# Longer expected waits around the decay products of the gated delta rule

## The chip, the core and the metric

The kernel runs on one core of one Trainium2 chip. TensorE multiplies matrices into PSUM; VectorE (DVE), ScalarE (ACT) and GpSimd (POOL) do the elementwise work; SyncE (SP) issues the loads. The engines run side by side and wait for one another on semaphores, and each takes its own instructions in the order in which the program lists them. The metric is the device time of one execution in microseconds (us), lower is better.

## The reference, cut to what matters

Two transformer blocks run on 512 tokens of width 1024 in float32. The first block mixes tokens with four groups of heads (softmax attention with a forget gate, gated delta rule, and two gated linear attentions), then a gated feed-forward; the second holds a short convolution, latent attention and two more feed-forwards. The change touches the gated delta rule:

```
G = jnp.cumsum(g.reshape(b, h, n, c), axis=-1)
decay = jnp.exp(jnp.where(causal, G[..., :, None] - G[..., None, :], -jnp.inf))
m = jnp.where(strict, jnp.einsum('bhnrd,bhnsd->bhnrs', kb, k) * decay, 0.0)
t_mat = m + jnp.eye(c, dtype=m.dtype)
w = lax.linalg.triangular_solve(t_mat, kb * jnp.exp(G)[..., None], ...)
u = lax.linalg.triangular_solve(t_mat, v * beta[..., None], ...)
a_qk = jnp.where(causal, jnp.einsum('bhnrd,bhnsd->bhnrs', q, k) * decay, 0.0)
```

After that a state of 64x64 per head goes from chunk to chunk. There are four heads, worked in two pairs.

## The kernel before, in words

All weights are float32 and are split into a high and a low part, so that a product is three matmuls per slice of 128 inputs (high by high, high by low, low by high). Such a triple is called a dense step here; a dense product of 128 output columns is eight of them. The token mixing stage takes the first 409 us and has 37 dense products: 29 that make the inputs of the heads (one of 29 named jobs each) and 8 of the output projection. It holds 296 dense steps, and between them stand the small matmuls of the heads.

TensorE's order in this stage is written by a planner in the kernel, `conduct` (L761). It runs once, when the program is built. Three lanes hold the heads' work as generators: lane G (the delta rule's pairs, here gdn0 and gdn1; PSUM tiles `gps`), lane L (hg0, gla, hg1: the gated linear attentions; `lps`) and lane F (fox0, fox1: softmax attention; `fps`). A generator issues some work and yields the time, by the planner's own clock, after which its next piece is expected to be ready. `conduct` adds the cost of every matmul that it writes to its clock. When a generator is due, its next piece is written; until then dense steps are. So a larger yield means that more dense steps stand between two pieces. The constants are LA = 0.68 and LV = 1.0 for one operation of ScalarE or VectorE. At run time the order is fixed, and a piece that is not ready holds up everything behind it on TensorE.

The order of VectorE, ScalarE and GpSimd is made by a scheduler from the same program, so it moves with TensorE's.

`gdn(p)` is the generator of one pair. It transposes k and q (L1059), then for each head j of the pair it writes the decay product (a masking matmul with `identb`, and four of `g` against a triangle, into one `gps` tile; the line of all `mm` calls is L708), ScalarE's exponential (tile `gmt`, L1091), the product of k and q and its weighting by VectorE (tile `gat`, L1034), the product of k and k and its weighting (`gmt`, L1034), and the start of the inverse (`u` L1113, `gxt` L1114). `gps` has two buffers. After both heads come six levels of block inversion (tiles `gy`, `gx`, `gxt`) and the chunk states (`gst`). `la` (L1325) is the generator body of lane L: seven levels, each with two copies per head into `lat` (L1371), products into `lbd` (L1320) and matmuls `lps<-lbd,lw`.

Three more rules matter. A job can be held until another piece is over: gv1, gk1 wait for gdn0's first half, gq1 for all of gdn0. Where a held job is not free, the next free one of the list is taken. And sigmoid-weighted inputs and gates (`silus`, L912) are collected, and a table load with a batch of activations follows only at jobs marked with a star in the list of jobs; gv1 has no star.

Of the kernel before, what the change touches and what calls it, by code (L numbers as in the profile page):

```python
# [648 lines left out]
LA, LV, LP = 0.68, 1.0, 1.5  # L649
# [17 lines left out]
class Mix(Mla):  # L667
# [371 lines left out]
    def gdn(self, p):  # L1039
# [34 lines left out]
        nc.vector.tensor_tensor(out=kof, in0=kof, in1=ik, op=ALU.mult)  # L1074
        nk = self.s1(8, "gnk", 2)
        nc.vector.tensor_tensor(out=nk, in0=ss[:, 8:16], in1=rr[:, 8:16], op=ALU.mult)
        yield 0.0
        MT, MR, AT, X, XT = [], [], [], [], []
        for j in range(2):
            rows = slice(64 * j, 64 * j + 64)  # L1080
            gp = self.pst()
            self.mm(c4(gp), self.identb, bc(self.negt), stop=False)
            for c in range(4):
                col = 4 * c + 2 * p + j
                self.mm(
                    gp[:, c * 128 : c * 128 + 128], self.g[:, col : col + 1].to_broadcast([128, 128]), self.triu,
                    start=False, stop=(c == 3),
                )
            e = self.b("gmt", bufs=2)
            for c in range(4):  # L1090
                nc.scalar.activation(  # L1091
                    out=e[:, c * 128 : c * 128 + 128], in_=gp[:, c * 128 : c * 128 + 128], func=ACTF.Exp,
                    bias=bias[:, 2 * c + j : 2 * c + j + 1],
                )
            yield Y_GDN / (1 + j)
            kp = self.pst()
            for c in range(4):
                cs = slice(c * 128, c * 128 + 128)
                self.mm(kp[:, cs], k[rows, cs], q[rows, cs])
            at = self.b("gat", bufs=2)  # L1100
            self.weighted(at, kp, ik, j, e)
            yield LV
            kp = self.pst()
            for c in range(4):
                cs = slice(c * 128, c * 128 + 128)
                self.mm(kp[:, cs], k[rows, cs], k[rows, cs])
            mt = e
            self.weighted(mt, kp, ik, j, e)
            mr = self.b("gmr", F32R, bufs=2)
            nc.scalar.activation(out=mr, in_=mt, func=ACTF.Copy)  # L1110
            xt = self.b("gxt", F32R, bufs=2)
            t1 = self.t(tag="s")
            nc.vector.tensor_tensor(out=c4(t1), in0=c4(mt), in1=bc(self.nm1), op=ALU.mult)  # L1113
            nc.vector.tensor_tensor(out=c4(xt), in0=c4(t1), in1=bc(self.ident), op=ALU.add)  # L1114
            MT.append(mt), MR.append(mr), AT.append(at), XT.append(xt)
            yield LV
        nc.gpsimd.tensor_tensor(out=d4(ke), in0=d4(ko), in1=b64(eG), op=ALU.mult)
        nc.gpsimd.tensor_tensor(out=d4(ko), in0=d4(ko), in1=b64(h2(kof)), op=ALU.mult)
        tp = self.to_tokens(v)
# [578 lines left out]
```

## Time and profile before

| what | value |
|---|---|
| median of three runs | 1855.37 us (1853.81 to 1861.0) |
| the profiled execution | 1864.82 us, span 1863.0 us |
| TensorE busy | 1825.5 us, 98% of the span |
| VectorE, ScalarE, GpSimd busy | 1051.9, 736.6, 190.3 us |
| mean granted TensorE clock | 0.989 |

The profile is one execution. A time in it is counted from the start of the span; "idle before" is the time that an engine stood still ahead of an instruction, with the instruction that released it; the granted clock is a share of TensorE's full speed of 2.4 GHz, so 0.50 is 1.2 GHz. Busy time of TensorE includes the modelled end of a matmul, which overlaps the next one, so the cost of a matmul in a stream is read from one start to the next.

### The profile page before, as it was taken

The page shows a single profiled execution, that of the slowest core. Times are in us where ns is not written, and L with a number is a line of the kernel's source. Part 1 is how long each engine was busy: PE and PEld are TensorE (multiplying, and loading weights), DVE is VectorE, ACT ScalarE, POOL GpSimd, SP SyncE. Part 2 cuts the span into 40 slices and gives each one's busy share as a digit, 9 for nine tenths or more (in the row PEclk, how much of TensorE's full clock was granted, in tenths as well). Part 3 has the DMA queues.
Part 4 walks back from the last instruction along what each step waited for, and adds up shares of the span by engine and source line. Part 5 has one row for each costly group of instructions (what it writes and reads, how often), then busy time and mean ns, then how long its engine had stood idle before and what let it go on. Part 6 is the DMA issues. An engine that isn't in the chain of part 4 may idle for free.

```text
span 1863.0 us, 22029 instructions
## 1 busy us (share of the span) xinstructions
PE 1825.5 (98%) x8609; PEld 1509.5 (81%) x8609; DVE 1051.9 (56%) x1620; ACT 736.6 (40%) x1138; POOL 190.3 (10%) x221
## 2 busy tenths in 40 slices
PE   8999999999999999999999999999999999999997
PEld 6787788878888888888888888888787888888886
DVE  7885966767777733455464444333876454444323
ACT  6544525554444422322342332222667433232322
POOL 1511402210000001011200000011011200000000
PEclk9999979999999999999999999999999999999999
DMA  4111101232222333222322222333222222222332
GB/s 167 57 46 35 57 23 35 97 99 102 91 102 92 96 94 95 99 102 91 102 96 102 91 101 92 93 101 98 70 61 74 79 91 102 95 98 92 100 94 76
DMA packets 53175, 162.61 MB, mean 87 GB/s; under 512 B 6480, under 2 KB 13136, under 8 KB 53072
## 3 DMA queue, kind: packets, MB, share of 16 engines
q1 hardware_dynamic: 52672, 160.95, 26.3%
q8 instruction: 67, 1.10, 0.2%
q14 instruction: 36, 0.29, 0.0%
q10 hardware_dynamic: 400, 0.27, 0.0%
HBM read 157.78 MB, written 2.10 MB: 86 GB/s over the span
## 4 chain that ended last, share of the span: by engine, by line
PE 85%; DVE 8%; ACT 3%; issue 1%; POOL 1%; DMA 0%; SPq 0%; DVEq 0%; POOLq 0%; ACTq 0%
PE mm L125 24%; PE mm L127 24%; PE mm L126 24%; PE mm L708 6%; PE gps L708 3%; PE lps L708 2%; PE fps L708 1%; ACT wh L111 1%; DVE lbd L1320 1%; DVE wl L112 1%; DVE lat L1371 1%; PE ps L580 0%; POOL s L1309 0%; DVE ptl L112 0%; PE ps L165 0%
## 5 line engine op out<-in xcount | busy, mean ns | idle before, releaser
L111 ACT ACTIVATE wh<-raw 128x1024 fp32r<-128x1024 f32 (+3 forms) x308 | 308.6, 1003 | 765.9 <-PE mm L126 434.0
L125 PE MATMUL mm<-xh,wh 128*128 128x512 f32 x1336 | 522.5, 391 | 0.5 <-ACT xh L173 0.5
L126 PE MATMUL mm<-xl,wh 128*128 128x512 f32 x1336 | 521.4, 390 | 0.5 <-DVE xl L174 0.5
L127 PE MATMUL mm<-xh,wl 128*128 128x512 f32 x1336 | 520.6, 390 | 0.0
L112 DVE TENSOR_TENSOR wl<-raw,wh 128x1024 fp32r<-128x1024 f32 (+3 forms) x300 | 362.3, 1208 | 225.4 <-ACT wh L111 222.4
L126 PEld LDWEIGHTS mm<-xl,wh 128*128 128x128 f32 x1336 | 251.0, 188 | 54.5 <-DVE xl L174 1.4
L125 PEld LDWEIGHTS mm<-xh,wh 128*128 128x128 f32 x1336 | 251.0, 188 | 53.4 <-issue 1.0
L127 PEld LDWEIGHTS mm<-xh,wl 128*128 128x128 f32 x1336 | 251.0, 188 | 52.0 <-issue 0.2
L125 PE MATMUL mm<-hidh,wh 128*128 128x512 f32 (+1 forms) x614 | 237.1, 386 | 0.0
L127 PE MATMUL mm<-hidh,wl 128*128 128x512 f32 (+1 forms) x614 | 235.5, 384 | 0.0
L126 PE MATMUL mm<-hidl,wh 128*128 128x512 f32 (+1 forms) x614 | 234.1, 381 | 0.0
L708 PE MATMUL mm<-xh,wh 128*128 128x512 f32 x291 | 129.4, 445 | 7.0 <-ACT xh L173 5.9
L127 PEld LDWEIGHTS mm<-hidh,wl 128*128 128x128 f32 x614 | 115.5, 188 | 24.1
L126 PEld LDWEIGHTS mm<-hidl,wh 128*128 128x128 f32 x614 | 115.5, 188 | 23.3
L125 PEld LDWEIGHTS mm<-hidh,wh 128*128 128x128 f32 x614 | 115.8, 189 | 21.8 <-ACT wh L111 0.2
L708 PE MATMUL mm<-xh,wl 128*128 128x512 f32 x291 | 117.4, 403 | 1.6 <-DVE wl L112 1.6
L708 PE MATMUL mm<-xl,wh 128*128 128x512 f32 x291 | 117.6, 404 | 0.4 <-DVE xl L112 0.4
L278 DVE TENSOR_TENSOR u<-mm,rb 128x512 f32<-128x512 f32 x44 | 30.4, 692 | 140.9 <-PE mm L127 140.9
L158 POOL TENSOR_TENSOR z<-z,sq 128x512 f32<-128x512 f32 x31 | 50.9, 1641 | 556.7 <-ACT sq L156 519.0
L274 DVE TENSOR_TENSOR u<-mm,rb 128x512 f32<-128x512 f32 x44 | 30.4, 691 | 90.9 <-PE mm L127 90.8
L111 ACT ACTIVATE hidh<-s 128x512 fp32r<-128x512 f32 x66 | 41.7, 632 | 88.3 <-DVE s L255 57.5
L708 PEld LDWEIGHTS mm<-xh,wh 128*128 128x128 f32 x291 | 56.9, 196 | 19.3 <-ACT xh L173 6.4
(433 smaller groups left out, 2093.9 us busy)
## 6 DMA issues: line engine op xcount, KB each, us to landing
raw<-in_w_a_dram SPq DMA_DIRECT2D x52, 512.0 KB, 3.3
raw<-in_w_b_dram SPq DMA_DIRECT2D x52, 512.0 KB, 3.2
raw<-in_w_up_dram SPq DMA_DIRECT2D x44, 512.0 KB, 3.2
raw<-in_w_in_dram SPq DMA_DIRECT2D x28, 512.0 KB, 3.3
raw<-in_conv_w_in_dram SPq DMA_DIRECT2D x24, 512.0 KB, 3.2
raw<-in_w_down_dram SPq DMA_DIRECT2D x16, 448.0 KB, 3.3
raw<-in_w_a_dram SPq DMA_DIRECT2D x16, 448.0 KB, 3.3
raw<-in_w_b_dram SPq DMA_DIRECT2D x16, 448.0 KB, 3.3
```

The costliest lines, as they stand in the source:

```text
L111: nc.scalar.activation(out=h, in_=src, func=ACTF.Copy)
L112: (eng or nc.vector).tensor_tensor(out=l, in0=src, in1=h.bitcast(F32), op=ALU.subtract)
L125: nc.tensor.matmul(out=ps, lhsT=h, rhs=xh, start=(k == 0), stop=False)
L126: nc.tensor.matmul(out=ps, lhsT=h, rhs=xl, start=False, stop=False)
L127: nc.tensor.matmul(out=ps, lhsT=l, rhs=xh, start=False, stop=(k == kt - 1))
L158: eng.tensor_tensor(out=acc, in0=acc, in1=sq, op=ALU.add)
L274: nc.vector.tensor_tensor(out=g, in0=ps, in1=r, op=ALU.mult)
L278: nc.vector.tensor_tensor(out=g, in0=ps, in1=r, op=ALU.mult)
L708: self.nc.tensor.matmul(out=out, lhsT=lhsT, rhs=rhs, start=start, stop=stop)
L1320: nc.vector.tensor_tensor(out=bd[rows, :, h].rearrange("p c (n j) -> p c n j", j=b), in0=c4(q)[rows], in1=c4(d)[rows], op=ALU.mult)
L1371: nc.vector.copy_predicated(out=at.rearrange("p c (n j) -> p c n j", j=2 * b)[:, :, :, b:], mask=self.lmask[:, lv - 1].rearrange("p (n j) ...
```

## The change

Two yields in `gdn` get other values. After the factors of the pair's rows are computed, ahead of the first decay product, the generator yields 2 * LA = 1.36 instead of 0.0. After the first head's products (j = 0), ahead of the second head's decay product, it yields 2.5 * LV = 2.5 instead of 1.0; after the second head's it still yields 1.0. Nothing that is computed changes.

```diff
@@ -1074,7 +1074,7 @@
         nk = self.s1(8, "gnk", 2)
         nc.vector.tensor_tensor(out=nk, in0=ss[:, 8:16], in1=rr[:, 8:16], op=ALU.mult)
-        yield 0.0
+        yield 2 * LA
         MT, MR, AT, X, XT = [], [], [], [], []
...
             MT.append(mt), MR.append(mr), AT.append(at), XT.append(xt)
-            yield LV
+            yield LV if j else 2.5 * LV
```

The first place on TensorE is gdn0, between the transposes of q and the first decay product (`mixb,identb`).

```order
 L715 MATMUL gps<-mlac,gq 128x128 x4
+L708 MATMUL mm<-xh,wh 128x512
+L708 MATMUL mm<-xl,wh 128x512
+L708 MATMUL mm<-xh,wl 128x512
...
 L708 LDWEIGHTS identb
 L708 MATMUL gps<-mixb,identb 128x512
```

Three dense steps (nine matmuls, of which three are shown) now stand where none stood. Ahead of the second decay product there were one dense step and a transpose after the k by k product; now there are two products of lane L and two dense steps, and four more dense steps follow it.

The second place is ScalarE's list in the middle of the stage, where the collected activations are written. Before, gv1 (the tile `gv`) goes with gq1:

```order
177 L226 ACTIVATE gq_1824<-z_1821,mixp_210 128x512
178 L261 ACT_TABLE_LOAD
179 L261 ACTIVATE gq_1824<-gq_1824 128x512
180 L261 ACTIVATE gv_1245<-gv_1245 128x512
181 L264 ACT_TABLE_LOAD
182 L111 ACTIVATE wh_1897<-raw_1895 128x1024
```

Now it goes with a gate, after gla's levels:

```order
203 L111 ACTIVATE wh_2088<-raw_2086 128x1024
204 L1389 ACTIVATE s_2306<-s_2306 128x512
205 L261 ACT_TABLE_LOAD
206 L261 ACTIVATE gate_2068<-gate_2068 128x512
207 L261 ACTIVATE gv_1937<-gv_1937 128x512
208 L264 ACT_TABLE_LOAD
```

Because gdn0's first half is over later in the planner's clock, a gate takes the place of gv1 in the jobs, and gv1 waits for the next star. gdn1 needs gv1, so it starts after dense step 177 of the stage where it started after step 150.

The third place is VectorE's list in the levels of gla. Before, gdn1's weightings (`gat`, `gmt`, `u`, `gxt`) stand between gla's copies and products:

```order
274 L1371 COPY_PREDICATED lat<-lmask,lps 128x4x32 x4
275 L1320 TENSOR_TENSOR lbd_227<-lq,s 32x4x64 x4
276 L1034 SCALAR_TENSOR_TENSOR gat<-gps,gik,gmt 128x128 x4
277 L1034 SCALAR_TENSOR_TENSOR gmt<-gps,gik,gmt 128x128 x4
278 L1371 COPY_PREDICATED lat<-lmask,lps 128x8x16
279 L1113 TENSOR_TENSOR u<-gmt,mixb 128x512
280 L1371 COPY_PREDICATED lat<-lmask,lps 128x8x16
281 L1114 TENSOR_TENSOR gxt<-u,mlac 128x512
282 L1371 COPY_PREDICATED lat<-lmask,lps 128x8x16 x6
```

Now the same levels hold only gla and the dense products' own rows:

```order
266 L1371 COPY_PREDICATED lat<-lmask,lps 128x4x32 x8
267 L1320 TENSOR_TENSOR lbd_227<-lq,s 32x4x64 x4
268 L904 TENSOR_TENSOR rq<-mm,rb 128x512
269 L112 TENSOR_TENSOR wl<-raw,wh 128x1024
270 L1371 COPY_PREDICATED lat<-lmask,lps 128x8x16 x8
271 L1320 TENSOR_TENSOR lbd_226<-lq,s 32x4x64 x4
272 L930 TENSOR_TENSOR gate<-mm,rb 128x512
273 L112 TENSOR_TENSOR wl<-raw,wh 128x1024
```

gdn1's weightings come after gla's last level and after fox1's normalisations (`sq`, `fq`, `fk`). gdn1's end moves from dense step 212 to step 240, beside hg1, which ran alone there.

## Rows read from the trace of the kernel before

**Rows 1.** The page: TensorE's busy time, and its granted clock in 40 slices
```profile
PE 1825.5 (98%) x8609; PEld 1509.5 (81%) x8609; DVE 1051.9 (56%) x1620; ACT 736.6 (40%) x1138; POOL 190.3 (10%) x221
...
PEclk9999979999999999999999999999999999999999
```

**Rows 2.** Waits of TensorE from 0 to 420 us: total us, times, longest
```profile
PE lps L708 <- DVE lat L1371: 1.7, 1, 1.7
```

**Rows 3.** Timeline of TensorE, the decay products of gdn0: start us, us, [idle before]
```profile
51.76 0.38 PE L708 MATMUL gps<-mixb,identb 128*128 128x512 bf16 x1 [1.06 <-ACT gko L1065]
51.98 1.05 PE L708 MATMUL gps<-mixc,gg 128*128 128x128 f32 x8
52.78 0.48 PE L708 MATMUL mm<-xh,wh 128*128 128x512 f32 x1
...
64.39 0.38 PE L708 MATMUL gps<-mixb,identb 128*128 128x512 bf16 x1 [1.51 <-DVE gat L1034]
```

**Rows 4.** Timeline of TensorE, the long idle times from 230 to 300 us
```profile
231.72 1.47 PE L708 MATMUL lps<-lbd,lw 128*128 128x256 f32 x4 [2.00 <-DVE gate L1025]
...
259.62 0.77 PE L708 MATMUL lps<-lst,lqi 128*128 128x128 f32 x2 [1.31 <-DVE lst L1411]
...
299.81 0.63 PE L708 MATMUL gps<-gxt,gy 128*128 128x64 f32 x4 [0.60 <-DVE gxt L1149]
```

**Rows 5.** Windows: us, busy PE, PEld, DVE, ACT, POOL, granted clock, DMA, GB/s
```profile
200.00:220.00 20.00, 20.00 (x107) 15.99 (x106) 19.73 (x62) 11.04 (x21) 11.05 (x9) 1.00 0.16 51
...
232.00:236.00 4.00, 4.00 (x16) 3.48 (x16) 2.87 (x9) 0.00 (x0) 0.00 (x0) 0.55 0.20 75
236.00:240.00 4.00, 4.00 (x15) 3.38 (x14) 1.75 (x5) 0.00 (x0) 0.52 (x1) 0.60 0.00 0
...
260.00:264.00 4.00, 4.00 (x18) 3.71 (x17) 2.19 (x6) 1.04 (x3) 0.31 (x1) 0.50 0.00 0
...
276.00:280.00 4.00, 4.00 (x18) 3.65 (x18) 1.78 (x5) 1.15 (x5) 0.00 (x0) 0.50 0.00 0
280.00:284.00 4.00, 4.00 (x16) 3.48 (x16) 1.99 (x7) 0.31 (x1) 0.00 (x0) 0.55 0.01 2
...
300.00:304.00 4.00, 4.00 (x16) 2.87 (x16) 3.45 (x5) 3.95 (x5) 3.38 (x3) 0.58 0.00 0
```

**Rows 6.** VectorE by line and shape, 0 to 420 us: xcount | busy us, mean ns
```profile
L1371 DVE COPY_PREDICATED lat<-lmask,lps 128x128 f32<-128x128 uint8 x48 | 13.2, 346 | 4.6 <-PE lps L708 4.6
...
L112 DVE TENSOR_TENSOR xl<-gate,xh 128x512 fp32r<-128x512 f32 x6 | 5.4, 914 | 0.0
...
L1034 DVE SCALAR_TENSOR_TENSOR gat<-gps,gik,gmt 128x128 f32<-128x128 f32 x16 | 4.5, 340 | 0.0
...
L1114 DVE TENSOR_TENSOR gxt<-u,mlac 128x512 fp32r<-128x512 f32 x4 | 3.2, 789 | 0.0
L1452 DVE SCALAR_TENSOR_TENSOR fq<-rq,fqg,sq 64x512 f32<-64x512 f32 x4 | 3.0, 747 | 0.1
...
L142 DVE TENSOR_TENSOR sq<-sq 128x512 f32<-128x512 f32 x4 | 2.8, 693 | 0.1
...
L1061 DVE TENSOR_REDUCE gss<-u 128x8 f32<-128x512 f32 x4 | 2.7, 680 | 0.8 <-ACT u L1060 0.8
...
L1002 DVE TENSOR_SCALAR fm<-fm 128x8 f32<-128x8 f32 x8 | 1.3, 166 | 0.1
```

**Rows 7.** Timeline of TensorE, the starts of gdn1's and gla's matmuls
```profile
193.56 1.03 PE L708 MATMUL lps<-lbd,lw 128*128 128x256 f32 x4
194.42 0.60 PE L715 MATMUL gps<-mlac,gk 128*128 128x128 f32 x4
...
203.37 1.16 PE L708 MATMUL gps<-gq,gk 64*128 64x128 f32 x8
204.45 0.50 PE L708 MATMUL mm<-xh,wh 128*128 128x512 f32 x1
...
206.03 1.16 PE L708 MATMUL gps<-gk 64*128 64x128 f32 x8
```

## The prediction

> **What bounds the kernel now.** I read the page first: TensorE is busy for 98% of the span [rows 1], so the time is TensorE's own work plus the moments in which it stands still or runs slow, and no other engine's total matters by itself. The clock row has one slice below 9 in 40, the sixth, a 7 [rows 1]. That slice lies in the token mixing stage, the only one that the change touches. The second view was the timeline of TensorE there, for its idle times. Two of them stand exactly ahead of the decay products of gdn0: 1.06 us until ScalarE has read the transposed k, and 1.51 us until VectorE has weighted the k by q product [rows 3]. Three more come later, 2.00, 1.31 and 0.60 us, all until VectorE has finished something [rows 4]. The third view was the table of windows around these: from 200 to 220 us VectorE is busy 19.73 of 20 us while TensorE still runs, so VectorE falls behind there, and the 2.00 us at 231.72 is that debt [rows 4, 5]. After each of the three later waits the granted clock falls to its lower level, 1.2 GHz: 0.55 and 0.60 in two windows after the first, 0.50 in five windows (the first and the last are shown) and 0.55 in one after the second, 0.58 in one after the third [rows 5]. In those windows TensorE loses 4 us times one minus the clock: 1.8 + 1.6 + 5 x 2.0 + 1.8 + 1.7 = 16.9 us. So at this place the slow clock costs more than the waits do (2.00 + 1.31 + 0.60 = 3.9 us).
>
> **The change part by part.**
>
> The first yield puts three dense steps ahead of gdn0's first decay product. Two dense steps take 1.58 us (204.45 to 206.03), so three take about 2.4 us [rows 7]. They are work that has to be done anyway. 2.4 us is more than the 1.06 us that TensorE waits there, so that wait goes: -1.06 us. What is late next is ScalarE's exponential, and seven dense steps follow as before, so nothing.
>
> The second yield puts, between the k by q product and the second decay product, a k by k product (1.08 us by its k by q twin, 203.37 to 204.45), two products of lane L of like size, three dense steps and a transpose [rows 7]. That is about 3.2 + 2.4 + 0.4 = 6.0 us, where before it was some 3.5 us of work and the 1.51 us wait, 5.0 us together [rows 3]. VectorE's list has two `lbd` rows moved ahead of `gat` there, which cost it 1 to 2 us. I take the margin as used up but for 0.3 us: -1.2 us. The two together are -2.3 us. Bounds: 0 if VectorE's moved rows eat all of it, -2.6 if none.
>
> No instruction is added or removed, and the same is true of DMAs. The larger part is what the order does next. gv1 loses its place and its activation is collected with a later batch, so gdn1 starts at dense step 177 and no longer at 150. What leaves VectorE's saturated stretch: two `gat` and two `gmt` of four instructions (4.5 us for 16 `gat`, so 1.1 us each time, 4.5 us in all), two `gxt` at 0.79 and two `u` of the same size (3.2 us): 7.7 us [rows 6]. What leaves TensorE's there: four products of 1.08 us and two decay products of 1.02 us (51.76 to 52.78), 6.4 us, but its dense steps close up, so it is TensorE's full work that paces that stretch [rows 3, 7]. VectorE was 98.7% busy over 20 us; 7.7 us less, and three rows of gv1's convolution in (0.75 us each by other three-operand rows of this shape, 2.2 us), leave it near 14 of 20. I therefore cost the 2.00 us wait at 0, with its two slow windows: -2.0 - 3.4 us. The 1.31 and 0.60 us waits stand where gla's state, fox1's normalisations and gdn1's inversion met; gla's state now comes some eight steps after the normalisations. I cost them at 0 too, with the 13.5 us of slow clock that follow them: -1.9 - 13.5 us. Together -20.8 us.
>
> Where the work comes back: between gdn1's transposes and its second decay product, VectorE has two `gss` (1.4 us), seven small rows (at 0.17 us, 1.2), sixteen copies of gla's last two levels (13.2 us for 48, so 4.4), six rows of fox1's normalisations (0.69 each, 4.1), four `fq` and `fk` (3.0) and one `gat` (1.1): 15.2 us, and it cannot begin before ScalarE has squared the transposes, which took about 2 us: 17 us [rows 6]. TensorE has there ten dense steps (7.9 us), four products of gla of 0.86 us (193.56 to 194.42), two products of 1.08, one decay product of 1.02: 14.5 us, and fox1's two sums and transposes beside them, which I put at 2 us: 16.5 us [rows 3, 7]. The two are even, so a wait of 0 to 4 us; I take 1.5 us, the size of the one at 64.39, and behind it one dip of the clock as long as the one behind the 2.00 us wait, 3.4 us: +4.9 us.
>
> The rule of the Trainium skill that speaks against this estimate is in "TensorE: Matmul & The Clock Gate", section "A second HAM failure mode: psum-queue depth-cycling": an engine that idles briefly but often between groups of matmuls has its clock drop and rise again, and pays for it between bursts. The trace agrees in part: 0.60 us at 299.81 was followed by 0.58, but 1.06 and 1.51 us in gdn0 were not followed by any low slice [rows 1, 3 to 5]. By the rule the 13.5 us would not go away with two single waits; that is the second case below, 1855 us.
>
> Sum against the profiled execution's own time: 1864.8 - 2.3 - 20.8 + 4.9 = 1846.6 us. This execution is 9.4 us above the median of the three runs, 1855.4. If that difference is slow clock that the timed runs had less of, the floor is the same and the changed kernel is timed at 1846.6; if it is something that every profiled execution has, the changed kernel is timed at 1837.2. The dip from 260 to 284 us alone (11.8 us) could account for it, so I give the first three parts in four: 1844 us, with 1837 to 1851 as this case's own range.
>
> **The rivals.**
>
> Second: only the waits in gdn0 go, and VectorE's debt is moved rather than paid. For it speaks that the 17 us against 16.5 are even at best, that the debt of the stretch before may still be there when they begin, and that a second dip like that from 260 to 284 needs one wait only. Then the sum has 11.8 us of slow clock where I put 3.4: 1846.6 + 8.4 = 1855 us; counted from the median with the gdn0 waits alone gone it is 1855.4 - 2.3 = 1853. This case covers 1848 to 1862. That the change does not do what it says for the second pair belongs here: gdn1's own decay products hardly waited before, so the yields give it nothing.
>
> Third, the slow one: gdn1's tail is now beside hg1 and beside the splits of the outputs that are already finished, at dense steps 228 to 240. VectorE's list has five such splits (0.91 us each, 4.6 us) and two `lbd` rows around the two corrections of gdn1's inverse, each of which TensorE needs at once [rows 6]. Before, the same burst met hg1 alone and cost one wait of 1.7 us [rows 2]. If TensorE waits for the whole burst and a dip of the long kind follows, that is 4.6 + 11.8 = 16.4 us on 1853: 1869 us. It decides from where the burst makes one wait of 2 us or more, as at 231.72. Against it: some four dense steps (3.2 us) and two products of hg1 stand between the corrections.
>
> **How the numbers follow.** Chances: 0.51 for my forecast, 0.33 for the second case, 0.16 for the third. About 0.5% is what a measurement of this kernel tells from no change, so faster means below 1846.1 and slower above 1864.6. Four fifths of the first case and a little of the second are faster, 0.43; the rest of the first and nearly all of the second are no change, 0.42; most of the third, 0.15, is slower. The range of 8 in 10 runs from 1836 (the floor of the first case) to 1866 (the lower part of the third).
>
> **What would show it.** The idle time ahead of `mixb,identb` in gdn0 gone or under 0.4 us, twice. VectorE below 18 of 20 us in the levels of gla (about 195 to 225 us), and no wait for `gate` L1025 of 1 us or more. A wait of 0 to 3 us for `gat` at gdn1's second decay product, about 230 us. At most two windows of 4 us with a clock under 0.7 between 200 and 310 us, where before there were nine. After 335 us, waits for `gy` or `gmr` of no more than 2 us in all. The forecast is wrong if the clock is low for 15 us or more anywhere in the stage, or if VectorE is still full in gla's levels without gdn1, for then it was gla itself and not the meeting of the two that held up TensorE.

## The result and the profile after

The changed kernel takes 1874.53 us (median of six runs, 1873.41 to 1877.37) where the kernel before takes 1855.46 beside it: a ratio of 1.0099, 95% interval 1.0082 to 1.0116, 19.1 us slower. The prediction was 1844 us, faster; the time lies outside its range of 1836 to 1866. The profiled execution of the changed kernel took 1875.0 us, with a span of 1873.2. The page, busy TensorE and its granted clock:

```profile
PE 1823.1 (97%) x8609; PEld 1506.5 (80%) x8609; DVE 1053.8 (56%) x1620; ACT 738.6 (39%) x1138; POOL 186.3 (10%) x221
...
PEclk9999999999999999999999999999999999999999
```

No engine's total moved by more than 4.0 us, and no slice of the clock row is low any more [rows 1]. By these two lines alone one would call this the better kernel. The timeline of TensorE in the mixing stage tells another story. First the places that answer to [rows 3] and [rows 4], then what is new:

```profile
52.58 0.39 PE L708 MATMUL gps<-mixb,identb 128*128 128x512 bf16 x1
...
68.44 2.07 PE L708 MATMUL lps<-lq,lk 64*128 64x128 f32 x8 [3.83 <-ACT lv L1278]
70.44 0.61 PE L708 MATMUL gps<-mixb,identb 128*128 128x512 bf16 x1
...
131.93 0.46 PE L715 MATMUL fps<-mlac,fp 128*128 128x128 f32 x1 [2.93 <-ACT fp L1473]
...
225.00 1.10 PE L708 MATMUL lps<-lbd,lw 128*128 128x256 f32 x4 [1.28 <-DVE lat L1371]
...
251.78 0.38 PE L708 MATMUL gps<-mixb,identb 128*128 128x512 bf16 x1
...
265.42 0.49 PE L708 MATMUL lps<-lst,lqi 128*128 128x128 f32 x2 [0.73 <-DVE lst L1411]
...
273.03 0.69 PE L708 MATMUL fps<-fv,fpt 128*128 128x64 f32 x2 [3.98 <-ACT fpt L1485]
...
305.00 0.88 PE L708 MATMUL fps<-fv,fpt 128*128 128x64 f32 x6 [2.48 <-ACT fpt L1485]
...
350.85 0.49 PE L708 MATMUL gps<-gvn,gko 128*128 128x128 f32 x2 [1.57 <-ACT gvn L1180]
...
368.03 0.63 PE L715 MATMUL gps<-mlac,u 128*128 128x128 f32 x4 [1.89 <-DVE u L1010]
...
370.16 0.50 PE L708 MATMUL mm<-xh,wh 128*128 128x512 f32 x1 [1.51 <-ACT xh L111]
```

Both waits ahead of gdn0's decay products are gone (52.58 and 70.44 have none), and the waits for VectorE at [rows 4] have shrunk: 2.00, 1.31 and 0.60 us are now 1.28 (for `lat`, in gla's levels), 0.73 and nothing. In their place stand five waits that ScalarE (ACT) ends: 3.83, 2.93, 3.98, 2.48 and 1.57 us, 14.8 us together. The windows (columns as in [rows 5]) show a low clock behind the four longest, and VectorE busy for 18.01 us from 200 to 220 where it was 19.73:

```profile
60.00:80.00 20.00, 16.16 (x81) 12.98 (x79) 14.25 (x27) 7.88 (x19) 11.70 (x10) 0.83 0.15 53
...
120.00:140.00 20.00, 17.07 (x94) 14.68 (x93) 11.51 (x29) 8.57 (x20) 0.72 (x3) 0.83 0.08 27
...
200.00:220.00 20.00, 20.00 (x90) 16.65 (x90) 18.01 (x40) 9.44 (x21) 6.64 (x8) 1.00 0.24 83
205.00:225.00 20.00, 18.72 (x86) 15.32 (x84) 18.96 (x42) 9.64 (x23) 7.01 (x8) 1.00 0.22 79
232.00:252.00 20.00, 19.17 (x98) 14.75 (x98) 19.73 (x53) 9.86 (x20) 3.88 (x5) 1.00 0.08 27
...
260.00:280.00 20.00, 15.29 (x86) 13.12 (x86) 12.01 (x30) 10.11 (x24) 1.83 (x4) 0.83 0.09 27
...
300.00:320.00 20.00, 17.52 (x103) 14.55 (x102) 10.73 (x21) 11.17 (x21) 4.44 (x5) 0.91 0.07 26
```

VectorE's full stretch has moved and not gone. gla's levels start some 10 us later now, at 204 us; VectorE is busy for 18.96 of 20 us in the first of them (205 to 225), and for 19.73 from 232 to 252, where their last ones meet fox1's normalisations and gdn1. TensorE waits little in that second stretch, 0.83 us once.

What did ScalarE do meanwhile? Its own timeline ahead of the ends of these five waits, with what it was waiting for in brackets:

```profile
67.18 0.42 ACT L1310 ACTIVATE s<-s 128x256 f32<-128x256 f32 x1 [2.74 <-POOL s L1309]
67.50 0.40 ACT L1311 ACTIVATE s<-s 128x256 f32<-128x256 f32 x1
67.80 0.58 ACT L1278 ACTIVATE lv<-lps 128x512 f32<-128x512 f32 x1
...
126.78 1.28 ACT L261 ACT_TABLE_LOAD   x1
129.38 0.63 ACT L261 ACTIVATE gk<-gk 128x512 f32<-128x512 f32 x1 [1.31 <-DVE gk L228]
130.03 1.28 ACT L264 ACT_TABLE_LOAD   x1
131.32 0.21 ACT L885 ACTIVATE finr<-fm 128x8 f32<-128x8 f32 x1
131.44 0.35 ACT L1473 ACTIVATE fp<-fps,nm 128x128 f32<-128x128 f32 x1
...
268.27 1.28 ACT L261 ACT_TABLE_LOAD   x1
269.56 1.15 ACT L261 ACTIVATE gate<-gate 128x512 f32<-128x512 f32 x2
270.73 1.28 ACT L264 ACT_TABLE_LOAD   x1
272.02 0.21 ACT L885 ACTIVATE finr<-fm 128x8 f32<-128x8 f32 x1
...
272.71 0.27 ACT L1485 ACTIVATE fpt<-fps 128x128 f32<-128x128 f32 x1
...
303.16 1.28 ACT L264 ACT_TABLE_LOAD   x1
304.46 0.49 ACT L1485 ACTIVATE fpt<-fps 128x384 f32<-128x384 f32 x1
...
348.38 1.28 ACT L264 ACT_TABLE_LOAD   x1
349.68 0.63 ACT L111 ACTIVATE xh<-gate 128x512 fp32r<-128x512 f32 x1
350.21 0.58 ACT L1180 ACTIVATE gvn<-gps 128x512 f32<-128x512 f32 x1
```

The last four of the five waits end with a small copy or exponential that stood behind a silu batch: a table load, the batch, and a load back. The first such batch keeps ScalarE from 126.78 to 131.31, 4.5 us, since the load runs at once and the silu then waits for VectorE; the second takes 3.7 us. Both kernels have nine batches in this stage. From the kernel before, places like those of the first, second and fourth of these waits:

```profile
66.64 0.58 ACT L1278 ACTIVATE lv<-lps 128x512 f32<-128x512 f32 x1
68.27 1.16 PE L708 MATMUL lps<-lq,lk 64*128 64x128 f32 x8
...
118.22 0.37 ACT L1473 ACTIVATE fp<-fps,nm 128x128 f32<-128x128 f32 x1
120.69 0.33 PE L715 MATMUL fps<-mlac,fp 128*128 128x128 f32 x1
...
304.40 0.49 ACT L1485 ACTIVATE fpt<-fps 128x384 f32<-128x384 f32 x1
305.38 0.78 PE L708 MATMUL fps<-fv,fpt 128*128 128x64 f32 x6
```

There, too, `fp` and `fpt` stood right behind batches, but they were done at 118.59 and 304.89, before TensorE came to what needs them. In the changed kernel TensorE came at 129.00 and 302.52, and they were done at 131.79 and 304.95. So what changed is when TensorE gets there. The softmax strands yield only 0.68 or 1.68 us between their pieces (LA, or LV + LA), less than any batch takes.

The first, 3.83 us for lv (hg0's transposed v), is another thing: hg0's second product needs the `lps` buffer that the copy of lv frees, and that copy stands in ScalarE's list behind eight exponentials of hg0's levels, which wait for GpSimd in turn (2.74 us at 67.18). In the kernel before it stood as far back and was done at 67.2, but the second product came later (68.27), after the wait for `gat` and two dense steps.

### The profile page after: what moved, and what is told of

It reads as the page before. It is cut to its first block, busy times and chain, and to the rows that moved or that the text cites. A ratio compares the mean times of both kernels' runs of the same rounds, so it can differ in the third digit from the quotient of the medians.

```text
span 1873.2 us, 22045 instructions
## 1 busy us (share of the span) xinstructions
PE 1823.1 (97%) x8609; PEld 1506.5 (80%) x8609; DVE 1053.8 (56%) x1620; ACT 738.6 (39%) x1138; POOL 186.3 (10%) x221
## 4 chain that ended last, share of the span: by engine, by line
PE 87%; DVE 6%; ACT 4%; issue 1%; POOL 1%; DMA 0%; SPq 0%; DVEq 0%; ACTq 0%; POOLq 0%
PE mm L125 24%; PE mm L127 24%; PE mm L126 24%; PE mm L708 8%; PE gps L708 2%; PE lps L708 2%; PE fps L708 1%; ACT wh L111 1%; DVE wl L112 1%; POOL s L1309 0%; PE ps L580 0%; DVE lat L1371 0%; DVE ptl L112 0%; DMA raw<-in_w_in_dram 0%; ACT L264 0%
## 5 line engine op out<-in xcount | busy, mean ns | idle before, releaser
L125 PE MATMUL mm<-xh,wh 128*128 128x512 f32 x1336 | 522.3, 391 | 0.2 <-ACT xh L173 0.2
L112 DVE TENSOR_TENSOR wl<-raw,wh 128x1024 fp32r<-128x1024 f32 (+3 forms) x300 | 366.6, 1222 | 224.7 <-ACT wh L111 220.9
L125 PEld LDWEIGHTS mm<-xh,wh 128*128 128x128 f32 x1336 | 251.0, 188 | 53.2 <-issue 1.0
L125 PE MATMUL mm<-hidh,wh 128*128 128x512 f32 (+1 forms) x614 | 237.0, 386 | 0.0
L125 PEld LDWEIGHTS mm<-hidh,wh 128*128 128x128 f32 x614 | 115.7, 189 | 21.7 <-ACT wh L111 0.2
```

The lines of the kernel that those rows point to most:

```text
L112: (eng or nc.vector).tensor_tensor(out=l, in0=src, in1=h.bitcast(F32), op=ALU.subtract)
L125: nc.tensor.matmul(out=ps, lhsT=h, rhs=xh, start=(k == 0), stop=False)
```

## The experiments

Every run can be put into one account. In each profile I added up TensorE's idle times from 30 us to the end of the mixing stage (the first matmul of line L125), and the slow clock, as 20 us times one minus the granted clock, over the windows of 20 us from 0 to 440. "Rest" is the stage's end less both.

| kernel | median us | waits | slow clock | stage end | rest |
|---|---|---|---|---|---|
| before (profiled at 1864.8) | 1855.5 | 12.7 | 17.2 | 403.2 | 373.3 |
| changed | 1874.5 | 25.6 | 13.8 | 413.5 | 374.1 |
| e1 first yield | 1861.0 | 14.6 | 5.2 | 394.2 | 374.4 |
| e2 second yield | 1864.4 | 19.4 | 7.0 | 402.1 | 375.7 |
| e3 change, old jobs | 1881.3 | 23.2 | 24.2 | 420.7 | 373.3 |
| e4 old yields, new jobs | 1874.5 | 23.3 | 13.8 | 413.0 | 375.9 |
| e5 change, lv first | 1873.5 | 24.0 | 10.4 | 410.0 | 375.6 |
| e6 change, no tables | 1855.9 | 15.9 | 3.6 | 395.3 | 375.8 |
| e7 before, no tables | 1852.2 | 10.2 | 5.4 | 389.5 | 373.9 |
| e8 first yield, lv first | 1855.0 | 13.8 | 3.6 | 392.3 | 374.9 |
| e9 change, fox put off | 1867.0 | 20.6 | 10.8 | 407.9 | 376.4 |
| e10 e9 and lv first | 1864.8 | 19.3 | 10.4 | 406.4 | 376.8 |
| e11 before, lv first | 1853.5 | 11.8 | 5.2 | 391.3 | 374.3 |
| e12 e8 and fox put off | 1856.4 | 15.7 | 3.6 | 394.7 | 375.4 |
| e13 change, loads kept | 1903.2 | 29.9 | 27.6 | 430.3 | 372.7 |
| e14 e3, no tables | 1870.4 | 17.3 | 8.6 | 399.1 | 373.2 |
| e15 e4, no tables | 1855.5 | 15.4 | 7.0 | 397.6 | 375.3 |
| e16 e11, finish waits for gate | 1856.3 | 14.8 | 3.4 | 394.3 | 376.0 |
| e17 e8, finish waits for gate | 1860.8 | 16.7 | 5.2 | 397.7 | 375.9 |
| e18 e10, finish waits for gate | 1864.8 | 21.4 | 5.4 | 404.0 | 377.2 |

The rest is 372.7 to 377.2 us in all twenty: but for those 4.5 us the work is the same, and the stage differs by its waits and its slow clock. The last four columns are of one profiled execution each, and the median is of all. They can lie apart: the profiled executions of e13 (1891.8 us), e14 (1861.5) and e1 (1856.2) are 11.4, 8.9 and 4.8 us under their medians. The executions of one kernel differ with the granted clock: e14's nine run from 1857.3 us at a mean of 0.996 to 1879.3 at 0.984. The kernel before was timed beside every set at 1853.9 to 1855.5 us.

**The two yields and the order of the jobs.** Only with both yields together is gdn0's first half late enough that gk1 is still held when its turn comes; gate gz0 is taken, and gk1 and gv1 move back. (So it is gk1's turn that the gate takes, and not gv1's, as the section on the change has it: the batch of gk1, at 116.28 before, is at 129.38 now, and one with a gate alone stands at 112.30.) e1 and e2 make one yield each, with the old order of jobs. e3 makes both and frees gk1 earlier; e4 leaves the yields and holds gk1 and gv1 longer.

```diff
# e3, in gdn, after the loop over j
+        self.over.add(f"gdn{p}.k")
-gk1="gdn0.kv"
+gk1="gdn0.k"
# e4, in gdn, at each level of the inversion
+            self.over.add(f"gdn{p}.l{lv}")
-gk1="gdn0.kv", gv1="gdn0.kv"
+gk1="gdn0.l1", gv1="gdn0.l1"
```

> Only the first yield of the change (2*LA ahead of the first decay product); the order of the jobs stays that of the kernel before. Order theory (the loss comes from gate gz0 taking the place of gk1, which moves the silu batches with their two table loads): no loss, 1855 us give or take 5, with the 1.06 us wait ahead of the first decay product gone. Yield theory (the longer waits themselves rob later products of their cover): about half of the loss or more, 1864 to 1874, with a wait of 2 us or more for lv, L1278, near 68 us.

Measured: 1861.0 us, 1.0041 (1.0024 to 1.0058).

> Only the second yield (2.5*LV after the first head); the order of the jobs stays that of the kernel before. Order theory: no loss, 1855 us give or take 5, with the 1.51 us wait ahead of the second decay product gone or under 0.5. Yield theory: about half of the loss or more, 1864 to 1874.

Measured: 1864.4 us, 1.0056 (1.0041 to 1.0071).

> Both yields, but product gk1 may start as soon as the second k by k product has been issued, which brings back the job order of the kernel before. Order theory: what is left is the 3.8 us wait for lv, L1278, at 68 us with its slow clock (1.7 us of a 20 us window at 0.83, so 3.4) against the 2.6 us gained: 1855 to 1862 us, no wait of 2 us or more for fp or fpt. Yield theory: as the changed kernel, 1870 to 1878.

Measured: 1881.3 us, 1.0157 (1.0125 to 1.0189).

> The yields of the kernel before, but gk1 and gv1 are held until gdn0's second level, which gives the job order of the changed kernel, gate gz0 ahead of gk1. Order theory: most of the loss, 1865 to 1875 us, with waits of 1.5 us or more for fp, fpt or gvn behind silu batches. Yield theory: 1855 us give or take 5.

Measured: 1874.5 us, 1.0133 (1.0100 to 1.0165).

Neither theory of the expectations holds. e4 gives the whole loss without a yield being changed, as the order theory has it. But e3 brings back the old jobs and is slower still, and each yield alone costs 7 and 10 us, against it. There is no one place: each order that is moved a little meets some late row. In e1 that is the copy of lv again:

```profile
65.72 0.38 PE L708 MATMUL gps<-mixb,identb 128*128 128x512 bf16 x1 [1.60 <-DVE gat L1034]
...
68.65 1.16 PE L708 MATMUL lps<-lq,lk 64*128 64x128 f32 x8 [1.66 <-ACT lv L1278]
```

The wait for `gat` stays, although three dense steps more stand ahead of it (1.51 us in [rows 3]), as the product that `gat` is made from moved back by as many. In this execution e1 has 1.9 us more of waits than the kernel before; its ten executions run from 1855.7 us (mean clock 0.996) to 1870.1 (0.987), so much of the 7 us is slow clock.

**ScalarE's list.** From here on the theory was that the new waits are rows that stand too far back in ScalarE's list, behind table loads or behind the levels' exponentials. Two tests: put the copy of lv ahead, with TensorE's order untouched (e5, e8, e11); and take the silu batches away (e6, e7, later e14, e15).

```diff
# lv first, in la (written shorter): hg0's levels, the later ones too, go behind the copy of lv
+        with ExitStack() as row:
+            if pair == 4:
+                row.enter_context(self.tc.issue_after(self.lvc))
             ws = [self.la_level(lv, q, k, g128, g16, es, nh) for lv in range(2)]
...
# no tables, in silus
-                ins = self.silu(y, y, i == n - 1)
+                ins = self.nc.scalar.activation(out=y, in_=y, func=ACTF.Copy).ins
```

> The changed kernel with TensorE's order untouched; only ScalarE's copy of hg0's transposed v (lv, L1278) is put ahead of the exponentials of hg0's levels, where it stood behind eight of them. ScalarE theory (the new waits are copies that stand too far back in ScalarE's queue): the 3.83 us wait at 68.44 falls under 0.5 and with it the slow clock behind it (20 us x 0.17 = 3.4), so 6 to 7 us: 1867 to 1870. The other new waits stay. VectorE theory (the list of VectorE is what holds the stretch): another wait of 1.5 us or more for gat or lat comes in its place, 1871 to 1876.

Measured: 1873.5 us, 1.0111 (1.0082 to 1.0140). The wait for lv is gone, but 1.05 us for `gat` at 77 and 1.30 us for `gvn` at 82 are new; the profiled stage ends 3.5 us earlier and the median is 1 us lower, not 6 to 7. The VectorE theory had this right.

> The changed kernel with every Silu of the mixing stage replaced by a plain copy on ScalarE (the sigmoid factor is left out), so that its eight pairs of table loads go; TensorE's order is the same. ScalarE theory: the waits for fp, fpt and gvn at 132, 273, 305 and 351 us (2.93, 3.98, 2.48, 1.57 us) all fall under 1 us, with the clock dips behind them (3.4 + 3.4 + 1.8): 1855 to 1860 us. If the softmax rounds are simply too short of dense steps, the waits stay within 1 us of what they were and the time is 1868 or more.

Measured: 1855.9 us, 1.0010 (0.9987 to 1.0033).

```profile
126.03 0.33 PE L715 MATMUL fps<-mlac,fp 128*128 128x128 f32 x1 [1.51 <-ACT fp L1473]
...
262.48 0.43 PE L708 MATMUL fps<-fv,fpt 128*128 128x64 f32 x2 [1.11 <-ACT fpt L1485]
```

Of the four waits behind batches (2.93, 3.98, 2.48, 1.57) 1.51 and 1.11 are left, and the other two are gone but for 0.19 us. "Under 1 us" was missed by half a microsecond; the time was not. (The batches are nine, not eight.)

> The kernel before with the same replacement of Silu by a copy (the sigmoid factor is left out). ScalarE theory: less to win than in the changed kernel, since only the waits of 2.00 us (gate, behind a batch at 226.6) and 1.73 us (lat, behind a batch at 351.5) lie behind a table batch: 1849 to 1854 us. If table loads cost the two kernels alike, it wins as much as the changed one does, 10 us or more: under 1845.

Measured: 1852.2 us, 0.9975 (0.9957 to 0.9992). Taking the table loads out is worth 18.6 us in the changed kernel and some 2 us in the kernel before. Without them the two are 3.7 us apart, where they were 19.1.

> The changed kernel with every Silu of the mixing stage replaced by a copy, as in the run without tables, but with the two table loads of each batch kept (one Silu of a single column between them). TensorE's order is the same. ScalarE theory: the loads are what TensorE waits behind, so most of the loss comes back, 1867 to 1875 us, with waits of 1.5 us or more for fp and fpt behind the batches. If the run without tables was faster because the lists of ScalarE and VectorE came out otherwise, 1854 to 1860 us.

```diff
+                ins = self.nc.scalar.activation(out=y, in_=y, func=ACTF.Copy).ins
+                if i == n - 1:
+                    with self.tc.issue_after(ins): ins = self.silu(self.dm, self.dm)   # one column
```

Measured: 1903.2 us, 1.0243 (1.0209 to 1.0276). This run is against the other reading of e6, that the scheduler merely wrote better lists without Silu (it did write other ones). With the loads back, the waits are back in their places (an edit makes the line numbers three higher here, and in e9):

```profile
136.88 0.48 PE L715 MATMUL fps<-mlac,fp 128*128 128x128 f32 x1 [4.43 <-ACT fp L1476]
...
289.60 0.69 PE L708 MATMUL fps<-fv,fpt 128*128 128x64 f32 x2 [4.05 <-ACT fpt L1488]
...
320.39 1.54 PE L708 MATMUL fps<-fv,fpt 128*128 128x64 f32 x6 [2.58 <-ACT fpt L1488]
...
367.72 0.49 PE L708 MATMUL gps<-gvn,gko 128*128 128x128 f32 x2 [1.68 <-ACT gvn L1183]
```

It overshot the 1867 to 1875 expected. Its profiled execution (1891.8 us) has 13.8 us of slow clock and 4.3 us of waits more than that of the changed kernel, and the other three are slower still, at a lower clock (0.977 and 0.978, against 0.984). Its lists are others again, so it shows where the waits come from, and not their price.

> The yields of the kernel before with the job order of the changed kernel (20 us over the kernel before), and every Silu of the mixing stage replaced by a copy, without table loads (the sigmoid factor is left out). ScalarE theory: 1853 to 1859 us, the waits for fpt (4.00, 1.37) and gvn (2.32) under 1.2 us each. If the job order costs by itself (gdn1 late, beside hg1): 1866 or more.

Measured: 1855.5 us, 1.0012 (0.9997 to 1.0027). So the new order of jobs costs 20.5 us with table loads (e4 over before) and 3.3 without (e15 over e7).

> Both yields with the job order of the kernel before (it was 27 us over the kernel before), and every Silu of the mixing stage replaced by a copy, without table loads (the sigmoid factor is left out). ScalarE theory: its waits for lst (2.70 us behind a batch at 115.0), rq (2.58 behind one at 307.7) and its 24 us of slow clock mostly go: 1853 to 1862 us. If the longer waits cost by themselves, whatever ScalarE does: 1868 or more.

Measured: 1870.4 us (1857.3 to 1879.3), 1.0080 (1.0049 to 1.0111). A miss for the theory: 11 us of e3's 27 go, the rest doesn't, and the median is in the range of the other theory. The wait of 2.70 us for lst, which I had put behind the batch, is still there without one:

```profile
115.79 0.49 PE L708 MATMUL lps<-lst,lqi 128*128 128x128 f32 x2 [2.70 <-DVE lst L1410]
```

It is VectorE's own: VectorE was busy without a break from 106 us until the copy into `lst` at 115.27. The spread of e14 is the clock's, as said at the table; why its clock falls for longer in some executions stays open, and so does what is left of e3's loss.

**Repairs.** e8 and e11 put the copy of lv ahead in kernels with the old order of jobs; e9 and e10 tell the planner of the batches, and e12 does so in e8; e16 to e18 also let a finish (the gating of a pair's output) wait for its gate.

```diff
# fox put off, in silus
+        for s in self.strands:
+            if s and s.name[:3] == "fox":
+                s.at = max(s.at, self.clk + LV + 2 * 1.28 + 0.63 * n)
# a finish waits for its gate
-        while gate and gate not in self.inp:
+        while gate and (gate not in self.inp or self.there[gate] > self.clk):
```

> The first yield alone, with the copy of lv put ahead as in the run of the changed kernel. ScalarE theory: the waits for lv (1.66 us) and, since VectorE's gat then comes ahead of two lbd rows, for gat (1.60 us) both fall under 0.5, and so does the dip (1.8): 5 us under the run with the first yield alone, 1850 to 1857 us. VectorE theory: lat or lbd is late in their place, 1858 to 1862.

Measured: 1855.0 us, 1.0004 (0.9995 to 1.0014): as expected, all of e1's loss goes when one ScalarE row moves ahead.

> The kernel before, its yields and TensorE's order as they are, with the copy of lv put ahead on ScalarE. The wait of 1.51 us for gat at 64.39 may shrink as VectorE gets one lbd row less ahead of its work for gdn0: 1851 to 1856 us. If the gap is VectorE's own, nothing changes, 1854 give or take 2.

Measured: 1853.5 us, 0.9996 (0.9975 to 1.0017). The wait at the second decay product falls from 1.51 to 0.53 us, too little to be timed.

> The changed kernel, and the planner told of the table loads: each time a silu batch is written down, the next step of a softmax strand (fox0 or fox1) is put off by LV + 2*1.28 + 0.63 for each silu of the batch. ScalarE theory: the waits for fp at 132 and for fpt at 273 and 305 us (2.93 + 3.98 + 2.48 = 9.4 us) fall under 1 us each, and with them most of the 8.6 us of slow clock behind them: 1857 to 1864 us. If the dense steps put there are missed somewhere else (the total of dense steps is the same), waits of like size come up in another place and the time is 1870 or more.

Measured: 1867.0 us, 1.0063 (1.0036 to 1.0090). The waits for `fp` and `fpt` fall from 9.4 us to 0.5, but the inversion of gdn1, beside fox1, now lacks the dense steps:

```profile
265.39 0.64 PE L708 MATMUL gps<-gx,gmr 128*128 128x64 f32 x4 [1.74 <-ACT gx L1127]
...
294.95 1.05 PE L708 MATMUL gps<-gx,gmr 128*128 128x64 f32 x4 [1.62 <-DVE gx L1149]
...
336.84 0.66 PE L708 MATMUL gps<-gxt,gy 128*128 128x128 f32 x4 [1.59 <-DVE gy L1163]
```

Of 9.4 us, 5.0 stay won (25.6 to 20.6 us of waits). The time lies between the two theories.

> The run before with the copy of lv put ahead as well. ScalarE theory: 1 to 7 us less than without it, 1852 to 1862 us; the sum of TensorE's waits between 30 us and the end of the stage under 17 us, where the changed kernel has 25.6. If cover is only moved about: over 20 us of waits, 1866 or more.

Measured: 1864.8 us, 1.0044 (1.0026 to 1.0061), 19.3 us of waits: a little under half of the loss is repaired, again between the two.

> First yield alone, copy of lv ahead, softmax strands put off behind silu batches. ScalarE theory: the two waits behind table batches that the run without it still had near fox1 and hg1 (1.75 for lat, 1.99 for gate) move or shrink: 1849 to 1855 us. If putting off costs cover elsewhere: 1857 or more.

Measured: 1856.4 us, 1.0026 (0.9999 to 1.0052): nothing won; the wait of 1.98 us for `gate` stays, and 2.00 us for `lat` come at 344.6.

> The kernel before, with the copy of lv put ahead on ScalarE, and a finish of a pair waits in the planner until its gate's silu is expected to be over, so that VectorE's gating row (gate, L1025) no longer stands in its list ahead of the silu's end. ScalarE theory: the waits of 2.02 us for gate at 231 and 1.72 us for lat at 344, which lie behind silu batches, fall under 0.7 each, with their dip: 1847 to 1852 us. If other rows come late in their place: 1853 or more.

Measured: 1856.3 us, 1.0011 (0.9998 to 1.0025). The waits for `gate` and `lat` do fall (2.02 to 0.82, 1.72 to nothing), and 1.93 us for `fpt` and 2.95 us for `u` come instead.

> The same two edits on the first yield alone. ScalarE theory: 1847 to 1853 us, no wait over 1.3 us behind a silu batch. If other rows come late: 1854 or more.

Measured: 1860.8 us, 1.0031 (1.0018 to 1.0043), in the range of the other rows: 1.81 us for `fpt` and 2.94 for `u` are there again.

> The changed kernel with all three edits (copy of lv ahead, softmax strands put off behind silu batches, a finish waits for its gate). ScalarE theory: a little under the run with two of them (1864.8), 1858 to 1864 us. If gating rows are not what holds VectorE there: 1864 or more.

Measured: 1864.8 us, 1.0055 (1.0039 to 1.0071), as without it. No version is faster than the kernel before by more than the interval, but the one without Silu, which leaves out work.

## Why the prediction was wrong, point by point

- **gdn0's two waits, -2.3 us.** Right that they go. Wrong in counting "two products of lane L of like size" as cover ahead of the second decay product: the second of them itself stood for ScalarE's copy of lv, 3.83 us with 3.4 us of slow clock (0.83 over 20 us). The place came to about +4.7 us (-1.06 - 1.51 + 3.83 + 3.4). Dense steps spent ahead of one piece are missing ahead of the next.
- **VectorE's saturated stretch, -20.8 us.** Its direction was right (19.73 to 18.01 us busy from 200 to 220; the wait for `gate` gone), its size was not: VectorE was near 19 of 20 us in gla's levels and not near 14, and full again from 232 to 252, so its debt was moved, as the second case has it. The waits of 2.00, 1.31 and 0.60 us, and one of 0.53 beside the last, became 1.28 and 0.73: -2.4 us instead of -3.9. The 16.9 us of slow clock did go, but that is luck for the larger part: the 11.8 us behind the wait of 1.31 us were in that one execution, and few are like it. (Its mean clock is 0.989; one of the 24 executions of this kernel timed beside e16, and four of the 31 beside e9, are at 0.989 or 0.990.) e11 has TensorE's order of the kernel before and the same wait of 1.31 us at 258.84, and its clock stays up there:

```profile
260.00:280.00 20.00, 20.00 (x137) 17.88 (x136) 17.17 (x46) 11.29 (x31) 0.62 (x2) 1.00 0.17 55
```

- **What comes back, +4.9 us: the step that failed.** It weighed VectorE's rows against TensorE's and found them even; the wait for `gat` at gdn1's second decay product, put at 1.5 us, did not come at all (251.78). Of ScalarE only the 2 us of squaring were in the sum, and no table load. Yet the order pieces showed the batch of gv1 moving, and the change made TensorE come to fox0's and fox1's rounds and to gdn1's tail while ScalarE was in four batches of 3.2 to 4.5 us: 11.0 us of waits (2.93 + 3.98 + 2.48 + 1.57) and 8.6 us of slow clock behind the first three (3.4 + 3.4 + 1.8), 19.6 us where +4.9 stood. By e6 and e7 15.4 us of the 19.1 go with the table loads (some of it is the copy of lv, which e6's lists put ahead); by e4, e7 and e15, where lv plays no part, 17 of 20.5.
- **The third case, slow, 1869 us.** Nearest in time, and its place is real: gdn1's tail beside the finished outputs waits 1.89 us for `u` and 1.51 for `xh`. Its mechanism (one burst of 4.6 us on VectorE and a long dip) is not what happened.
- **The rule of the Trainium skill** ("TensorE: Matmul & The Clock Gate", section "A second HAM failure mode: psum-queue depth-cycling"). It was to decide whether 13.5 us of slow clock stay. The dip of 11.8 us behind the wait of 1.31 us is neither in the changed kernel nor in e11, e1 or e8. What did stay in those three is 0.91 over 20 us behind the pair of 0.53 and 0.60 us, so a pair of short waits costs 1.8 us there, and not 13.5. Brief idling followed by a lower clock is what the rule of the Trainium skill describes; its price was not what the second case took it for.
- **The signs named.** "The forecast is wrong if the clock is low for 15 us or more anywhere in the stage, or if VectorE is still full in gla's levels" did not catch it. No dip of the changed kernel is that long, and VectorE is short of full. (At 18.96 of 20 us in gla's levels it is near it, and the wait of 1.28 us for `lat` there is one that gdn1 has no part in.) Most of the other signs came true: no wait for `gate`, none ahead of `mixb,identb` or for `gat`, two windows of 4 us with a clock under 0.7 between 200 and 310 us, at 272 and 276. They all looked at the engines of the sum, and the time went to the one that was not in it.

Against the profiled execution of before the account is +12.8 us of waits, -3.4 of slow clock and +0.8 of rest, 10.3 us at the stage's end. The median moved by 19.1, as the profiled execution of before was 9.4 above its median. For a usual execution e11 is the better measure (1853.5 us, TensorE's order of before): against it the changed kernel has 13.8 us more of waits and 8.6 us more of slow clock. So about two fifths of the loss, by this estimate, is the clock that falls behind the waits.

The Trainium skill, "ScalarE: Activation LUTs", section "Table sets: the hidden batching unit", says to batch activations by set so as to save loads. The kernel does so, and the number of batches did not change. The runs add that, with the number fixed, the place of a batch counts as well: e4 has nine as the kernel before has and is 20.5 us slower, and without table loads (e15 over e7) 3.3 us of that are left.

## What to carry to other kernels

Where one order feeds several in-order engines, balance each of them over the stretch that a change moves, the idle one too: ScalarE was 39% busy here, and its blocks of 3 to 4.5 us set the time. Before costing a delay at nothing, list what was waiting just behind it, for cover is moved, not made: repairs of 9.4 us gave back half. And take a slow clock in a single profiled execution as that execution's until a second one shows it.

## What the runs showed of the hardware

A table load does not wait for the data of the activation behind it: at 126.78 it ran, and the silu stood until 129.38 for VectorE, with the whole queue behind. The load costs 1.28 us and nothing more in these rows: the silu of the batch at 268.27 began 1.29 us later (269.56). The clock fell behind each of the four waits of 2.48 us and more in the changed kernel, but one of 1.31 us was followed by 0.50 over 260 to 280 us in one execution and by 1.00 in another of the same TensorE order. Nor is a longer wait enough: in e16 one of 2.95 us for `u` ended at 332.88, and the granted clock is 1.00 in every window of 4 us from 328 to 360. What decides is not shown.
